# Half chunks and a split root at the head, recurrence gating on GpSimd, a last half scaled from PSUM: a two-layer hybrid diffusion backbone on one core

## The chip, the cores and the metric

The kernel runs on one core of a Trainium2 chip. The metric is device microseconds of one execution on that core, the median of several runs. The program's core has TensorE (PE) for matrix products, VectorE (DVE), ScalarE (ACT), GpSimd (POOL) and SyncE (SP); here SP only issues the transfers. Everything is fp32 in and out.

## The reference, cut to what matters

512 latent tokens and 256 context tokens of width 1024 pass through two layers, and the latent tokens are normalised at the end:

```python
for layer in range(2):
    shift, scale, gate = split(silu(c) @ ada_w[layer] + ada_b[layer])        # and the same for c_ctx
    h_l = rmsnorm(x, norm_g[layer]) * (1 + scale) + shift                    # h_c likewise
    if layer == 0: y_c, y_l = even_mixer(h_c, h_l)   # latent attention | bidirectional RG-LRU
    else:          _,   y_l = odd_mixer(h_c, h_l)    # neighbourhood attention
    x = x + gate * y_l                                                       # cx likewise in layer 0
return rmsnorm(x, final_norm_g)

# even_mixer: z = h @ w_in -> cq, ckv, k_rope, gate_mla, x_lru, gate_lru
q, k, v = heads(rmsnorm(cq) @ w_uq), heads(rmsnorm(ckv) @ w_ukv), ...        # rope on a part of q and k
u = short_conv(x_lru); a, w = coeffs(u); r = scan_forward(a, w) + scan_backward(a, w)
y = concat(attend(q, k, v) * silu(gate_mla), r * silu(gate_lru)) @ w_out
# odd_mixer: q, k, v, g = split(h @ w_in); 8x16 window + context, then (o * silu(g)) @ w_out
```

## The kernel before, in words

Activations stand transposed: a tile holds 128 of the 1024 channels for 768 tokens, the 512 latent ones first (`LAT`), the 256 of the context behind them (`CTX`). Every fp32 product is made of three products of rounded parts: a value is split into a high part (an ACT copy, `h`) and the rest (a DVE subtraction, `l`), and `h·h`, `h·l`, `l·h` are summed in PSUM. `split_w` loads a weight (`r`) and makes `h` and `l`. A recording layer and a scheduler set the order of instructions on each engine; the text of the program gives priorities, and `behind()` makes an instruction stand after the last one recorded for TensorE.

Five places of the program are touched.

The head. `x_load` brings in eight tiles of x (384 KB each). `norm0` squares them on ACT, sums the squares on DVE in `acc`, multiplies by ones on TensorE (`pssum`), takes the root on ACT (`r0t`) and a Newton step on DVE (`r0r`, L302 to L306), spreads the result over partitions by six transposes (`r0b`) and copies it to SBUF (`rsb`). Meanwhile `ada_go(ch)` computes shift and scale of two channel tiles at a time from four loads of 512 KB (`ada_0r`, `ada_4r`; TensorE `psada`, ACT `rows`, TensorE `psc`, DVE `av`, `as`, `am`). `hb(j, c)` then makes the normalised `hh`, `hl` of tile j: x·am·rsb on DVE (L330), the high part on ACT (L332), the rest on DVE (L333). The first products with the layer's weights (`psx`, `w0t0`) use them.

Layer 0's middle. `lru_x`, `lru_conv`, `lru_gates` and `lru_scan` are the recurrence for four blocks `ft`, `natural` makes cq, ckv and k_rope (`psn`, weights `w0n0` to `w0n3`), and `ada_gate(0, 0)`, called as `g00`, makes half of the layer's output gate (`psada` again). `lru_out(ft)` multiplies the gate `mix` by the recurrence: the context part contiguous (L584), the latent part in two strided views (L586). `gate_t` makes such a gate (L445 and L446).

Keys and values of layer 0. `prep_q` and `prep_kv` load and split `wq0`, `wq1` and `wkv`, `rope_q` turns q (`rb` by a shuffle, `ra`, a product on GpSimd at L712, a sum at L713, the parts `qrh` and `qrl`), `k_rope` makes the rotated key `kh`, `kl` (L670 to L673), `v_t` the values (`psv`, L689), `proj_k` the keys (`psk`).

The start of layer 1. `v_t1`, `q1` and `g1` make values, queries and gates; `prep1("w1g", 0)` loads and splits the gate's first weight. `pskl` are the keys.

The tail. The last output product (`w1oy`, L1144) is added to x (`out_add`, L1150), squared (L1697) and summed, for two halves of 256 tokens. `norm2(half)` makes the root `r2` and its spread copy `rsb2`, `finish(half)` multiplies and issues the output's transfers on SP (L1671 to L1674). Half 0's tiles have been multiplied by the final weight before (L1699); of half 1, those in `GF`.

## Time and profile before

| what | value |
|---|---|
| runs | 790.94 us median of 3 (790.9 to 793.72) |
| the profiled execution | 792.74 us, of which the span is 790.9 us |
| PE busy | 742.5 us, 94% of the span |
| DVE, ACT, POOL busy | 511.1, 415.4, 151.7 us |
| chain that ended last | PE 78%, DVE 11%, ACT 5%, issue 2%, DMA 2% |
| granted TensorE clock, mean | 0.991 |

The span is the time from the first to the last instruction; the execution's own time has 1.84 us more. An engine's busy time is summed over its instructions; the chain is followed back from the last instruction to what released each. Of TensorE's clock the profile gives the granted share, 1.00 for 2.4 GHz and 0.50 for 1.2 GHz.

### The profile page before, as it was taken

The numbers are of one execution on the slowest core, as the hardware profiler recorded it, in microseconds if no ns is written. First come the engines' busy times: TensorE is split into PE (matmuls) and PEld (weight loads), VectorE is DVE, ScalarE is ACT, GpSimd is POOL, SyncE is SP. The second block draws the span as 40 slices with busy tenths as digits, with TensorE's granted clock in tenths as the row PEclk, the third lists the DMA queues.
The fourth block names the chain that finished last, engine by engine and source line by source line (L and its number), as shares of the span: only waits on it lengthen the run. The fifth ranks groups of instructions, "written<-read, shape, count | busy, mean of one in ns | idle before, by whom it ended". The sixth has DMA issues, their size and how long they took to land.

```text
span 790.9 us, 13125 instructions
## 1 busy us (share of the span) xinstructions
PE 742.5 (94%) x4934; PEld 651.9 (82%) x4934; DVE 511.1 (65%) x1055; ACT 415.4 (53%) x806; POOL 151.7 (19%) x177
## 2 busy tenths in 40 slices
...
GB/s 326 407 43 107 63 116 102 159 42 0 110 144 148 179 166 143 96 158 273 28 80 107 80 160 15 89 112 187 56 79 156 165 107 54 124 89 164 78 1 107
DMA packets 33599, 95.29 MB, mean 120 GB/s; under 512 B 4608, under 2 KB 6784, under 8 KB 33536
## 3 DMA queue, kind: packets, MB, share of 16 engines
...
q14 instruction: 24, 0.20, 0.1%
...
## 4 chain that ended last, share of the span: by engine, by line
PE 78%; DVE 11%; ACT 5%; issue 2%; DMA 2%; SPq 1%; DVEq 0%; ACTq 0%
PE psg L140 11%; PE psv L1239 8%; PE w0oy L1144 7%; PE psq L140 6%; PE w1oy L1144 6%; PE pskl L140 6%; PE psx L140 4%; PE pt L1356 4%; PE pskc L140 3%; PE psn L611 3%; PE psada L210 2%; PE s L1315 2%; PE s L777 2%; PE s L1316 2%; PE po L1339 2%
## 5 line engine op out<-in xcount | busy, mean ns | idle before, releaser
L733 POOL TENSOR_SCALAR p<-p,rc 128x512 f32<-128x512 f32 (+1 forms) x96 | 77.7, 812 | 335.1 <-DVE rc L732 319.1
L1323 ACT ACTIVATE p<-s,nm 128x512 f32<-128x512 f32 x64 | 43.8, 686 | 36.4 <-DVE nm L1321 20.2
L1359 DVE TENSOR_TENSOR ptl<-pt,pth 128x512 fp32r<-128x512 f32 x64 | 43.7, 687 | 26.8 <-ACT pth L1358 26.8
L1358 ACT ACTIVATE pth<-pt 128x512 fp32r<-128x512 f32 x64 | 37.3, 595 | 34.8 <-PE pt L1356 25.6
L1321 DVE CUSTOM_DVE_ANT_1 s<-s,bias 128x512 f32<-128x512 f32 x48 | 33.2, 696 | 16.3 <-PE s L1316 16.1
L1356 PE MATMUL pt<-ident,p 128*128 128x128 f32 x256 | 40.0, 272 | 0.0
L813 DVE TENSOR_TENSOR pt<-pt,pt 128x512 fp32r<-128x512 f32 x48 | 31.8, 680 | 11.5 <-ACT pt L812 11.2
L712 POOL TENSOR_TENSOR rb<-rb,ropet 128x512 f32<-128x512 f32 x2 | 2.6, 1287 | 186.9 <-DVE rb L710 186.9
L812 ACT ACTIVATE pt<-pt 128x512 fp32r<-128x512 f32 x48 | 27.4, 595 | 16.1 <-PE pt L850 15.9
L732 DVE RECIPROCAL rc<-rs 128x1 f32<-128x1 f32 x96 | 15.2, 158 | 31.4 <-ACT p L1323 22.0
L1315 PE MATMUL s<-k,q 128*128 128x256 f32 x128 | 34.2, 292 | 0.6 <-ACT mix L1298 0.5
L210 PE MATMUL psada<-ada_0r,c 128*32 128x256 f32 x192 | 19.9, 407 | 15.7 <-DMA ada_0r<-ada 15.7
L781 ACT ACTIVATE p<-s,nm 128x768 f32<-128x768 f32 x32 | 28.8, 901 | 10.6 <-DVE nm L779 10.4
L1356 PEld LDWEIGHTS pt<-ident,p 128*128 128x128 f32 x256 | 31.1, 140 | 4.0 <-issue 0.4
L779 DVE TENSOR_REDUCE nm<-s 128x1 f32<-128x768 f32 x32 | 30.4, 951 | 4.7 <-PE s L777 4.3
L1316 PE MATMUL s<-k,q 128*128 128x256 f32 x128 | 33.3, 284 | 0.0
L1339 PE MATMUL po<-pth,v 128*128 128x256 f32 (+1 forms) x96 | 31.6, 336 | 0.0
L1340 PE MATMUL po<-ptl,v 128*128 128x256 f32 (+1 forms) x96 | 29.5, 324 | 0.0
L850 PE MATMUL pt<-ident,p 128*128 128x128 f32 x192 | 28.7, 274 | 0.0
L831 PE MATMUL po<-pt,v 128*128 128x256 f32 x96 | 26.1, 296 | 1.8 <-DVE pt L813 1.6
L830 PE MATMUL po<-pt,v 128*128 128x256 f32 x96 | 26.6, 294 | 0.4 <-DVE rcc L732 0.4
L1315 PEld LDWEIGHTS s<-k,q 128*128 128x128 f32 x128 | 24.3, 190 | 3.1 <-issue 1.0
...
## 6 DMA issues: line engine op xcount, KB each, us to landing
...
```

Of the source, the lines that this page charges most:

```text
L140: P.matmul(ps, a(k), b[k][:, c], start=(k == 0 and i == 0), stop=(k == nk - 1 and i == 2),)
L210: P.matmul(ps[32 * j : 32 * j + 32, :256], c34[:, k, 2 - 2 * m : 34 - 2 * m], raw[k // step][:, k % step], start=(m == 0 and k < 4), stop= ...
L733: G.tensor_scalar(p, p, rc, 0.5, ALU.mult, ALU.mult)
L1144: P.matmul(ps, a, b[k][:, c], start=(n == m == 0 and ps is dst[0][0]), stop=(n == 7 and m == 2), skip_group_check=True,)
L1239: P.matmul(ps, tok(a[k], t), b[:, k % 4], start=(k == 0 and i == 0), stop=(k == 7 and i == 2))
L1315: P.matmul(s[:, :256], lhs, kap, start=(i == 0), stop=False, skip_group_check=True)
L1316: P.matmul(s[:, 256:], lhs, k2[:, CTX], start=False, stop=(i == 1), skip_group_check=True)
L1323: S.activation(p, s, AF.Exp, bias=nm, scale=-1.0, accum_out=rsum)
L1339: P.matmul(dst, vv, h, start=first, stop=False, skip_group_check=True)
L1356: P.transpose(ps[:, 128 * j : 128 * j + 128], p1[hd, b][:, 128 * c : 128 * c + 128], ident)
L1358: S.activation(h, ps, AF.Copy)
L1359: V.tensor_tensor(l, ps, f(h), ALU.subtract)
```

## The change

At the head the first two channel tiles get their shift and scale each by itself, from a new input array `ada0` that holds the same weights in halves of 128 columns; the sum of squares and the root are made for the latent and the context tokens apart, the latent ones first (`r00`, `r01`); and a root of one column that nothing uses stands among the squares. The gate chunk `g00` is called earlier, around `lru_gates(0)`. The multiplications of `lru_out`, the sum in `rope_q` and a copy in `k_rope` go from DVE to GpSimd, and `prep_kv` stands ahead of `prep_q(0)`. In layer 1, `prep1("w1g", 0)` stands ahead of one `v_t1` and of the query weight. In the tail half 0 is finished on GpSimd alone and its eight products with the final weight are made on ACT behind its root; half 1 reads its spread root from PSUM on DVE; a root that nothing uses stands ahead of the tail; `finish` follows each `norm2`, and the odd tiles' transfers of half 1 are issued by ACT.

```diff
...
     V.tensor_scalar(badd, col(V_ADAB, 48), 1.0, None, ALU.add)
-    def behind():
-        e = next(i for i in reversed(nc.cur_bb.bb.instructions) if i.engine == mybir.EngineType.PE)
-        return tc.issue_after(e)
-    def ada_mm(raws, pp, name):
+    def behind(*engines):
+        stack = ExitStack()
+        for e in engines:
+            stack.enter_context(tc.issue_after(next(i for i in reversed(nc.cur_bb.bb.instructions) if i.engine == e)))
+        return stack
+    def ada_mm(raws, pp, name, wd=256):
...
-                    ps[32 * j : 32 * j + 32, :256], c34[:, k, 2 - 2 * m : 34 - 2 * m], raw[k // step][:, k % step],
+                    ps[32 * j : 32 * j + 32, :wd], c34[:, k, 2 - 2 * m : 34 - 2 * m], raw[k // step][:, k % step],
...
-    def ada_rows(l, ch, raws, pp, pin):
-        with behind() if pin else nullcontext():
+    def ada_rows(l, j, raws, pp, pin, na=2):
+        wd = 128 * na
+        with behind(PE) if pin else ExitStack():
...
-        with behind() if pin else nullcontext():
-            for i in range(2):
+        with behind(PE) if pin else ExitStack():
+            for i in range(na):
...
-    def ada_cols(l, ch, raws, pp, pin=False):
+    def ada_cols(l, j, raws, pp, pin=False, n=2):
...
         V.scalar_tensor_tensor(y, t, 1.5, y, ALU.add, ALU.mult)
-    def rs_bc(name, ps, n, dst, pp, root=True):
+    def rs(name, ps, n, root=True):
         nt = n // 128
         s, r = ps[:, 0 : 2 * nt : 2], small("st", f"{name}r", nt)
-        if root:
-            rsqrt1(r, s, 1.0 / D, nt, name)
-        else:
-            rsqrt(r, s, 1.0 / D, nt, "st", name)
+        (rsqrt1 if root else lambda *a: rsqrt(*a[:4], "st", a[4]))(r, s, 1.0 / D, nt, name)
+        return r
+    def bc(name, r, n, dst, pp):
         b = pp(f"{name}b")
-        for i in range(nt):
+        for i in range(n // 128):
             P.transpose(b[:, 128 * i : 128 * i + 128], r[:, i : i + 1].to_broadcast([128, 128]), ident)
         S.activation(dst[:, :n], b[:, :n], AF.Copy)
+        return b[:, :n]
+    def rs_bc(name, ps, n, dst, pp, root=True):
+        return bc(name, rs(name, ps, n, root), n, dst, pp)
     def halves(ap):
...
     rsb0 = px.tile([128, NT], F32, name="rsb0")
+    acc0 = px.tile([128, NT], F32, name="acc0")
+    root = cst.tile([128, 1], F32, name="root")
     def norm0():
-        acc = th("acc0")
-        ps = zz3("pssum")
+        sq = {}
         for j in range(8):
-            sq = th(f"sq{j}")
-            S.activation(sq, x_tiles[j], AF.Square)
-            if j == 0:
-                prev = sq
-            else:
-                V.tensor_tensor(acc, prev if j == 1 else acc, sq, ALU.add)
-        sq_sum(ps, acc, NT, True, True)
-        rs_bc("r0", ps, NT, rsb0, zz3)
+            sq[j] = th(f"sq{j}")
+            S.activation(sq[j], x_tiles[j], AF.Square)
+            if j == 4:
+                S.activation(root, sq[0][:, 0:1], AF.Sqrt)
+            for w in (LAT, CTX) if j == 7 else (slice(0, NT),):
+                if j:
+                    V.tensor_tensor(acc0[:, w], (acc0 if j > 1 else sq[0])[:, w], sq[j][:, w], ALU.add)
+                if j == 7:
+                    c = w is CTX
+                    n, pp = (NL, NC)[c], (zz, zz3)[c]
+                    ps = pp(f"pssum{c}")
+                    sq_sum(ps, acc0[:, w], n, True, True)
+                    if c == 0:
+                        rs_bc("r00", ps, n, rsb0[:, w], pp)
+                    else:
+                        norm0c = lambda: rs_bc("r01", ps, n, rsb0[:, CTX], pp)
+        return norm0c
     wt = {}
...
     def ada_go(ch):
-        for _ in ada_cols(0, ch, [ada_w.pop(ch), ada_w.pop(ch + 4)], paa):
+        for _ in ada_cols(0, 2 * ch, [ada_w.pop(ch), ada_w.pop(ch + 4)], paa):
+            pass
+    def ada_prep1(j):
+        ada_w["half", j] = [[load_w(f"ada0{j}{m}", A["ada0"][j, m], (8, 128), t4a)] for m in range(2)]
+    def ada_go1(j):
+        for _ in ada_cols(0, j, ada_w.pop(("half", j)), paa, n=1):
             pass
...
         x_load(j)
-    ada_prep(0)
-    ada_prep(4)
-    norm0()
+    ada_prep1(0)
+    norm0c = norm0()
     hh = [th(f"hh{j}", F32R) for j in range(8)]
     hl = [th(f"hl{j}", F32R) for j in range(8)]
-    ada_prep(1)
-    ada_go(0)
+    raw0 = load_w("w0t0", A["w0t"][0], (8, 128))
+    ada_prep1(1)
+    ada_go1(0)
     hb(0, 0)
-    prep_t(0)
-    hb(0, 1)
+    norm0c()
+    with behind(PE, ACT):
+        wt[0] = kfun(split_raw("w0t0", raw0, (8, 128)))
+        hb(0, 1)
+        ada_prep(1)
+        ada_go1(1)
+    hb(1, 0)
+    hb(1, 1)
     ada_prep(5)
-    hb(1, 0)
     ada_prep(2)
     ada_go(1)
-    hb(1, 1)
     ada_prep(6)
...
         g, r = mix[4 + ft], lru_s.pop(ft)["r"]
-        V.tensor_tensor(g[:, CTX], g[:, CTX], r[:, :NC], ALU.mult)
+        G.tensor_tensor(g[:, CTX], g[:, CTX], r[:, :NC], ALU.mult)
         for a, b in zip(in_cols(g), in_rows(r[:, NC:])):
-            V.tensor_tensor(a, a, b, ALU.mult)
+            G.tensor_tensor(a, a, b, ALU.mult)
     def lru_sqrt(i):
...
         S.activation(KH[1][64:96], f(KH[0][64:96]), AF.Copy)
-        V.tensor_copy(KL[1][64:96], f(KL[0][64:96]))
+        G.tensor_copy(KL[1][64:96], f(KL[0][64:96]))
     def prep_kv():
...
         G.tensor_tensor(rb[:, :NL], rb[:, :NL], ropet[0][:, 1], ALU.mult)
-        V.tensor_tensor(ra[:, :NL], ra[:, :NL], rb[:, :NL], ALU.add)
+        G.tensor_tensor(ra[:, :NL], ra[:, :NL], rb[:, :NL], ALU.add)
         S.activation(ra[:, NL:], psa[:, NL:NT], AF.Copy)
...
     lru_conv(1)
+    go("g00", ada_gate(0, 0, tt))
     lru_gates(0)
+    go("g00")
     lru_x(2, x_t(2))
     lru_gates(1)
-    go("g00", ada_gate(0, 0, tt))
-    go("g00")
     lru_conv(2)
...
     lru_scan(2)
+    prep_kv()
     prep_q(0)
...
     rope_q(0)
-    prep_kv()
     k_rope()
...
     v_t1(0, 1)
+    prep1("w1g", 0)
     v_t1(0, 2, st)
...
     q1(0, st)
-    prep1("w1g", 0)
     g1(0)
...
         return pe.tile([128, 256], F32, tag=tag, name=name, bufs=bufs)
-    GF = (1, 4, 6)
+    GF = (2, 6)
     steps = ((0, 0), (0, 2), (0, 4), (0, 6), (1, 0), (1, 2), (1, 4), (1, 6))
+    S.activation(root, p1[15, 3][:, 0:1], AF.Sqrt)
     acc2 = [etmp(f"acc2{half}", "acc", 2) for half in range(2)]
...
             if half == 0 or j in GF:
-                (V if half == 0 and j % 2 else G).tensor_tensor(x, x, rsb2[half], ALU.mult)
+                G.tensor_tensor(x, x, rsb2[half], ALU.mult)
             else:
-                V.scalar_tensor_tensor(x, x, col(V_FG + j), rsb2[half], ALU.mult, ALU.mult)
-            SY.dma_start(out[128 * j : 128 * j + 128, c], x)
+                V.scalar_tensor_tensor(x, x, col(V_FG + j), rb2[half], ALU.mult, ALU.mult)
+            (S if half and j % 2 else SY).dma_start(out[128 * j : 128 * j + 128, c], x)
+    rb2 = {}
     def norm2(half):
...
         sq_sum(pss[half], sq2[half], 256, False, True)
+        yield
+        r = rs(f"r2{half}", pss[half], 256)
+        if half == 0:
+            with behind(ACT):
+                for j in range(8):
+                    S.activation(x2[j][:, :256], x2[j][:, :256], AF.Copy, scale=col(V_FG + j))
         rsb2[half] = etmp(f"rsb2{half}", "rsb", 2)
-        rs_bc(f"r2{half}", pss[half], 256, rsb2[half], tt)
+        rb2[half] = bc(f"r2{half}", r, 256, rsb2[half], oo)
+        finish(half)
     sq2 = {}
...
             dst[1] = (st("w1oy71")[:, :256], 1)
-        for d in [[d] for d in dst] if (half, j0) == (1, 6) else [dst]:
-            out_mm(d, w1o[j0 // 2], mh, ml, [0, 3, 5, 2, 4, 1, 6, 7], c)
+        ks = [0, 3, 5, 2, 4, 1, 6, 7]
+        if (half, j0) == (1, 6):
+            for d in dst:
+                with behind(PE):
+                    out_mm([d], w1o[3], mh, ml, ks, c)
+                next(n2, None)
+        else:
+            out_mm(dst, w1o[j0 // 2], mh, ml, ks, c)
         for ps, i in dst:
...
             S.activation(sq, x2[j][:, c], AF.Square)
-            if half == 0 or j in GF:
+            if half and j in GF:
                 S.activation(x2[j][:, c], x2[j][:, c], AF.Copy, scale=col(V_FG + j))
             if 0 < j < 7:
-                (V if half else G).tensor_tensor(acc, acc, sq, ALU.add)
+                (V if half or j > 3 else G).tensor_tensor(acc, acc, sq, ALU.add)
         sq2[half] = sq
-        if (half, j0) == (1, 2):
-            norm2(0)
-    finish(0)
-    norm2(1)
-    finish(1)
+        if (half, j0) == (1, 4):
+            n2 = norm2(0)
+            next(n2)
+    for _ in norm2(1):
+        pass
     while pools:
...
     A["ada"] = ada_w.reshape(2, 8, 128, 12, 256).transpose(0, 3, 2, 1, 4)
+    A["ada0"] = ada_w[0].reshape(8, 128, 3, 8, 128)[:, :, :2, :2].transpose(3, 2, 1, 0, 4)
     def cols(a):
...
```

Three places of the resulting order. The first is TensorE's, in the products of `lru_gates` (`pg`, weights `lgh` and `lgl`) and of `natural` (`psn`). Before:

```order
L140 MATMUL pg_708<-ul_625,lgh_658 128x256
L140 MATMUL pg_708<-uh_624,lgl_660 128x256
L611 MATMUL psn_946<-w0n0l,hh_188 128x416
L611 MATMUL psn_946<-w0n0h,hl_196 128x416
L140 MATMUL pg_779<-uh_652,lgh_774 128x512
L140 MATMUL pg_779<-ul_653,lgh_774 128x512
```

and of the change:

```order
L141 MATMUL pg_756<-uh_664,lgl_708 128x256
L215 MATMUL psada_16_767<-ada_8_0r,c_109 32x256 x4
L215 MATMUL psada_16_767<-ada_8_4r,c_109 32x256 x4
L215 MATMUL psada_16_767<-ada_9_0r,c_109 32x256 x4
L215 MATMUL psada_16_767<-ada_9_4r,c_109 32x256 x4
L141 MATMUL pg_846<-uh_692,lgh_841 128x512
L141 MATMUL pg_846<-ul_693,lgh_841 128x512
```

The gate chunk's products (`psada_16`) now stand right ahead of the first product with the second block's `lgh`; before they stood some 60 rows further on. The second place is DVE's, from the gate of block 2 to the values; here `mix_1773` before and `mix_1813` in the change are the gate of block 3 (`gate_t(11, 7)`), `mix_1695` and `mix_1735` that of block 2. Before:

```order
L584 TENSOR_TENSOR mix_1695<-mix_1695,la_1229 128x256
L586 TENSOR_TENSOR mix_1695<-mix_1695,la_1229 128x8x48
L586 TENSOR_TENSOR mix_1695<-mix_1695,la_1229 128x8x16
L124 TENSOR_TENSOR wkvl<-wkvr,wkvh 128x1024
L446 SCALAR_TENSOR_TENSOR mix_1773<-mix_1773,psg_1724 128x768
L658 SCALAR_TENSOR_TENSOR cql_1806<-pscq_1814,vec,cqh_1805 128x256
L710 STREAM_SHUFFLE rb_1833<-psqr_1819 128x512
L711 TENSOR_TENSOR ra_1832<-psqr_1819,ropet 128x512
L584 TENSOR_TENSOR mix_1773<-mix_1773,la_1325 128x256
L586 TENSOR_TENSOR mix_1773<-mix_1773,la_1325 128x8x48
L586 TENSOR_TENSOR mix_1773<-mix_1773,la_1325 128x8x16
```

and of the change, on DVE:

```order
L477 SCALAR_TENSOR_TENSOR mix_1735<-mix_1735,psg_1686 128x768
L689 SCALAR_TENSOR_TENSOR cql_1751<-pscq_1752,vec,cqh_1750 128x512
L689 SCALAR_TENSOR_TENSOR cql_1751<-pscq_1759,vec,cqh_1750 128x256
L125 TENSOR_TENSOR wq1l<-wq1r,wq1h 128x512
L477 SCALAR_TENSOR_TENSOR mix_1813<-mix_1813,psg_1764 128x768
L689 SCALAR_TENSOR_TENSOR cql_1852<-pscq_1853,vec,cqh_1851 128x512
L689 SCALAR_TENSOR_TENSOR cql_1852<-pscq_1860,vec,cqh_1851 128x256
L741 STREAM_SHUFFLE rb_1879<-psqr_1865 128x512
L742 TENSOR_TENSOR ra_1878<-psqr_1865,ropet 128x512
```

and on GpSimd, where before only the product of `rb` stood at this place:

```order
L615 TENSOR_TENSOR mix_1735<-mix_1735,la_1269 128x256
L617 TENSOR_TENSOR mix_1735<-mix_1735,la_1269 128x8x48
L617 TENSOR_TENSOR mix_1735<-mix_1735,la_1269 128x8x16
L615 TENSOR_TENSOR mix_1813<-mix_1813,la_1365 128x256
L617 TENSOR_TENSOR mix_1813<-mix_1813,la_1365 128x8x48
L617 TENSOR_TENSOR mix_1813<-mix_1813,la_1365 128x8x16
L743 TENSOR_TENSOR rb_1879<-rb_1879,ropet 128x512
L744 TENSOR_TENSOR ra_1878<-ra_1878,rb_1879 128x512
L704 CAST kl_1892<-kl_1891 32x768
```

The six products of the two blocks left DVE, and on GpSimd they stand ahead of the two operations of the rope. The third place is DVE's in the tail, where `x_8058` before and `x_8098` in the change hold the last two tiles. Before:

```order
L1150 SCALAR_TENSOR_TENSOR x_8058<-w1oy_8635,ag_117,x_8058 128x256
L1701 TENSOR_TENSOR acc_8211<-acc_8211,sq_8686 128x256
L1671 TENSOR_TENSOR x_8049<-x_8049,rsb_8563 128x256
L1671 TENSOR_TENSOR x_8052<-x_8052,rsb_8563 128x256
L1671 TENSOR_TENSOR x_8055<-x_8055,rsb_8563 128x256
L1671 TENSOR_TENSOR x_8058<-x_8058,rsb_8563 128x256
L1150 SCALAR_TENSOR_TENSOR x_8058<-w1oy_8636,ag_117,x_8058 128x256
```

and of the change:

```order
L1181 SCALAR_TENSOR_TENSOR x_8098<-w1oy_8653,ag_119,x_8098 128x256
L1748 TENSOR_TENSOR acc_8252<-acc_8252,sq_8742 128x256
L1181 SCALAR_TENSOR_TENSOR x_8098<-w1oy_8654,ag_119,x_8098 128x256
L305 TENSOR_SCALAR r21m<-pss_8749 128x2
L306 RECIPROCAL r21r<-r21t 128x2
```

Half 0's four products no longer stand between the last sum of squares and the last tile's addition.

## Rows read from the trace of the kernel before

**Rows 1.** Windows by stage: length, busy us (instructions) of each engine, PEclk, DMA share, GB/s.

```profile
80.00:100.00 20.00, 17.18 (x113) 13.86 (x112) 11.96 (x17) 16.24 (x26) 0.00 (x0) 1.00 0.26 85
...
180.00:200.00 20.00, 15.40 (x75) 12.31 (x74) 18.87 (x30) 9.22 (x15) 1.28 (x1) 0.91 0.11 28
...
440.00:748.00 308.00, 307.05 (x2058) 275.45 (x2057) 187.45 (x406) 155.62 (x327) 53.35 (x68) 1.00 0.35 107
...
770.00:791.00 21.00, 8.91 (x69) 8.33 (x67) 11.35 (x29) 5.61 (x13) 6.00 (x7) 0.74 0.29 101
```

**Rows 2.** Timeline of PE at the head: start, length, instruction, idle before and releaser.

```profile
25.61 0.79 PE L140 MATMUL psx<-hh,w0t0h 128*128 128x512 f32 x2 [0.56 <-ACT hh L332]
...
35.78 0.50 PE L140 MATMUL psx<-hh,w0t0h 128*128 128x512 f32 x1
```

**Rows 3.** Timeline of ACT at the head.

```profile
19.36 1.28 ACT L301 ACT_TABLE_LOAD   x1 [4.37 <-PE pssum L290]
```

**Rows 4.** Timeline of DVE at the head.

```profile
24.05 2.20 DVE L330 SCALAR_TENSOR_TENSOR x<-x,am,rsb 128x512 f32<-128x512 f32 x4
...
32.13 2.20 DVE L330 SCALAR_TENSOR_TENSOR x<-x,am,rsb 128x512 f32<-128x512 f32 x4
```

**Rows 5.** Timeline of PE from 80 to 100 us.

```profile
86.03 0.50 PE L140 MATMUL pg<-uh,lgh 128*128 128x512 f32 x1 [0.92 <-ACT lgh L532]
...
91.26 0.65 PE L611 MATMUL psn<-w0n1h,hh 128*128 128x416 f32 x2 [0.96 <-ACT w0n1h L120]
```

**Rows 6.** Timeline of SP: the transfer of the second of `natural`'s weights.

```profile
86.73 0.33 SPq L114 DMA_DIRECT2D w0n1r<-w0n  x1
```

**Rows 7.** Timeline of PE from 182 to 200 us.

```profile
187.47 0.58 PE L140 MATMUL psk<-cqh,wkvh 128*128 128x512 f32 x2 [1.97 <-DVE mix L446]
...
195.14 0.50 PE L689 MATMUL psv<-wkvh,cqh 128*128 128x512 f32 x1 [2.13 <-DVE kl L671]
```

**Rows 8.** Timeline of DVE from 183 to 193 us.

```profile
183.77 0.42 DVE L584 TENSOR_TENSOR mix<-mix,la 128x256 f32<-128x256 f32 x1
184.11 1.22 DVE L586 TENSOR_TENSOR mix<-mix,la 128x384 f32<-128x384 f32 x2
185.24 1.22 DVE L124 TENSOR_TENSOR wkvl<-wkvr,wkvh 128x1024 fp32r<-128x1024 f32 x1
186.37 0.95 DVE L446 SCALAR_TENSOR_TENSOR mix<-mix,psg 128x768 f32<-128x768 f32 x1
...
191.75 0.68 DVE L713 TENSOR_TENSOR ra<-ra,rb 128x512 f32<-128x512 f32 x1
```

**Rows 9.** GpSimd's groups by line and shape: busy us, mean ns, idle before.

```profile
L1671 POOL TENSOR_TENSOR x<-x,rsb 128x256 f32<-128x256 f32 x7 | 6.0, 885 | 12.8 <-ACT rsb L319 12.8
...
L1701 POOL TENSOR_TENSOR acc<-acc,sq 128x256 f32<-128x256 f32 x6 | 4.4, 740 | 21.2 <-ACT sq L1697 20.8
L712 POOL TENSOR_TENSOR rb<-rb,ropet 128x512 f32<-128x512 f32 x2 | 2.6, 1287 | 186.9 <-DVE rb L710 186.9
```

**Rows 10.** Window from 196 to 200 us, columns as in rows 1.

```profile
196.00:200.00 4.00, 4.00 (x14) 3.15 (x13) 3.94 (x7) 2.84 (x5) 0.00 (x0) 0.57 0.55 137
```

**Rows 11.** Waits of PE from 400 to 440 us: total us, times, longest.

```profile
PE pskl L140 <- DVE v L1243: 1.4, 1, 1.4
PE psg L140 <- ACT w1g0h L120: 1.0, 1, 1.0
```

**Rows 12.** Timeline of DVE in the tail.

```profile
776.25 3.02 DVE L1671 TENSOR_TENSOR x<-x,rsb 128x256 f32<-128x256 f32 x4 [0.74 <-ACT rsb L319]
779.19 0.47 DVE L1150 SCALAR_TENSOR_TENSOR x<-w1oy,ag,x 128x256 f32<-128x256 f32 x1
...
783.53 3.56 DVE L1673 SCALAR_TENSOR_TENSOR x<-x,vec,rsb 128x256 f32<-128x256 f32 x5 [1.20 <-ACT rsb L319]
```

**Rows 13.** Timeline of ACT in the tail.

```profile
775.83 0.39 ACT L319 ACTIVATE rsb<-r20b 128x256 f32<-128x256 f32 x1 [0.24 <-PE r20b L318]
779.70 0.42 ACT L1697 ACTIVATE sq<-x 128x256 f32<-128x256 f32 x1 [3.48 <-DVE x L1150]
```

More of the change, by code (lines that the diff above doesn't have):

```diff
@@ L1 @@
-from contextlib import nullcontext
+from contextlib import ExitStack
 import numpy as np
@@ L52, in build @@
     V, S, P, G, SY = nc.vector, nc.scalar, nc.tensor, nc.gpsimd, nc.sync
+    PE, ACT, DVE = mybir.EngineType.PE, mybir.EngineType.Activation, mybir.EngineType.DVE
     def f(ap):
@@ L177, in build @@
     ctt = cst.tile([128, 8, 2], F32, name="ctt")
+    eps = cst.tile([128, 1], F32, name="eps")
+    G.memset(eps, EPS)
     S.activation(ctt, ct, AF.Tanh, scale=0.5)
```

32 lines of the change are left out of this document (15 added, 17 removed).

## The prediction

> **What bounds the kernel now.** I read the windows by stage first, to see where TensorE is not full, since the change takes nothing from its products. From 440 to 748 us it is busy 307.05 of 308 us, but it idles 2.82 of 20 us from 80 to 100, 4.60 from 180 to 200, and 12.09 of the last 21 [rows 1]. Time can only come from such gaps and from the head. So I then read, stretch by stretch, the timeline of PE with the releaser of each wait. At the head the first product with a weight starts at 25.61, and tile 2's at 35.78, after which no wait stands out [rows 2]; what goes before is the root, with a table load of 1.28 us in its chain [rows 3], and DVE, which starts on x at 24.05 [rows 4]. From 80 to 100 PE waits 0.92 us for a gate weight and 0.96 for `w0n1h` [rows 5], whose load is issued only at 86.73 [rows 6]. From 180 to 200 it waits 1.97 us for the gate of block 3 and 2.13 for `kl` [rows 7], and there DVE is busy 18.87 of 20 us [rows 1]: each is late because DVE works off a queue. At layer 1's start there are two waits, of 1.4 and 1.0 us [rows 11]. In the tail the last tile's addition runs at 779.19, behind four products of half 0 that take 3.02 us beside GpSimd [rows 12].
>
> **The sum is made against the profiled execution**, 792.74 us, which is 790.9 us of span and 1.84 around it. The median of the runs shown is 1.80 us below it, and I subtract the same gains from the median.
>
> **The head.** Until the first product two loads of 512 KB are wanted instead of four, and two small chains `av`, `as`, `am` replace one. The table load, 1.28 us [rows 3], goes ahead of the squares, where ACT waits for x. The latent sum needs eight of twelve products, and its copy has 512 columns instead of 768. If all of it reached the path, PE would start 2.5 us earlier. But DVE starts on x at 24.05 and is full until it starts on tile 2 at 32.13, 8.1 us later [rows 4]; the second small chain puts about 1 us more into that queue. With the new order and the old durations I get the first product at 24.0 instead of 25.61, tile 2's at 34.8 instead of 35.78, and some 0.2 us given back at the next shift and scale, which has less work ahead of it. Gain **0.8**, between 0.2 and 2.5.
>
> **The gate chunk.** 32 products of `psada`, 1.9 us by my count of its rows' starts, now stand ahead of the products with the second `lgh`, so they cover the 0.92; the load of `w0n1` no longer waits for the chunk's place in memory, which covers the 0.96 [rows 5, 6]. Of the stage's 2.82 us the rest is two waits for ACT of about 0.5 each. The chunk's sum holds one of three PSUM places of `pg` until ACT has copied it, which I put at 0.9 given back, and the stage's small waits go as well. On SP its four loads stand ahead of the next `lgr` loads, which wait for their places anyhow. Gain **1.7**, between 0 (the PSUM place costs as much as is saved) and 2.8 (all the idle time).
>
> **The gating on GpSimd.** Ahead of the gate of block 3 DVE no longer does block 2's three products, 183.77 to 185.24, and one `cql` of about 0.65 moves behind it; `wkvl` stays ahead, only earlier. The multiplication moves from 186.37 to about 184.2 and ends at 185.1 [rows 8], before PE is at `psk`, so that the wait of 1.97 goes. The second wait decides, because everything behind it moves with `kl`. GpSimd can start on block 2 when DVE ends that block's gate. Between that and block 3's stand two `cql` and `wq1l` (about 1.7), so at about 182.5. Then stand six products, the product of `rb` and the sum of `ra`. GpSimd takes 0.74 us for 256 columns and 1.29 for 512 [rows 9], which makes a contiguous block 0.74 + 1.0 + 0.46 = 2.2. No row shows it on strided views. DVE takes 0.42 for the contiguous 256, and 1.22 for the 512 strided, where it takes 0.68 contiguous [rows 8], partly from the GpSimd beside it; with 1.5 for the strided part the block is 2.9, and 3.5 when 0.74 grows to 0.885 as in the tail [rows 9]. I take 2.9, between the ends. The sum of `ra` is then at 182.5 + 2 × 2.9 + 2 × 1.29 = 190.9, where DVE's now ends at 192.43 [rows 8]. From there to `psv` at 195.14 are 2.71 us of `qrh`, `qrl` and `kl`, which stay, so `psv` starts at 193.6. Gain **1.5**; 2.5 with 2.2 us for a block (the shuffle then decides), 0.3 with 3.5. The copy of `kl` on GpSimd has nobody waiting soon; with that cover gone it costs under 1 us.
>
> The Trainium skill (GPSIMD Engine Reference, section 4.1, Engine selection) speaks against this part: two-input elementwise work is about 2 times slower on GpSimd than on VectorE. The rows agree, 1.29 against 0.68 for 512 columns [rows 8, 9]. By twice DVE's 0.42 + 1.22 a block would be 3.3 us, the gain 0.7 instead of 1.5 and the whole 784.
>
> **Layer 1.** Splitting the gate's weight earlier meets the wait of 1.0; the wait of 1.4 for a split on DVE keeps its values' products right ahead of it [rows 11]. Work moved ahead of the query weight can be late in its place. Gain **0.6**, between -0.5 and 1.5.
>
> **The tail.** ACT's root has its table loaded in an idle stretch of ACT. Eight products with the final weight, about 0.45 each, go behind half 0's root; they and the missing table load leave the copy of `rsb` about where it is, 775.83 [rows 13], so GpSimd starts its eight products at about 775.6 and ends at 781.5 with 0.74 each, at 782.7 with 0.885 [rows 9]. DVE has lost the four products (3.02), so the last addition follows TensorE's last product at about 777, with one sum of squares that may run beside GpSimd: the square starts at 777.4 instead of 779.70 [rows 13], 2.3 earlier. From that square to DVE's first product are 3.83 us now, 779.70 to 783.53 [rows 12, 13], of which 0.4 is the copy that DVE no longer waits for: DVE starts at 780.8. Six products of about 0.45, the length of the addition that reads PSUM now [rows 12], end at 783.4. GpSimd does its two of half 1 behind the eight and ends between 783.0 and 784.4. Now DVE ends at 787.09, 3.56 after 783.53 [rows 12]. What follows, transfer and end, stays at 3.8. The gain is 2.7 to 4.1; I take **3.3**.
>
> The Trainium skill (SBUF — State Buffer, section SBUF: two separate sides) says that a VectorE operation with two SBUF inputs and a GpSimd operation that reads SBUF exclude each other for a whole instruction. The trace agrees where half 0's four products take 0.76 each beside GpSimd, and 0.42 alone [rows 8, 12]. By it `wq1l` could wait one GpSimd product, 0.74, and the sum would be about 0.3 less.
>
> **The sum.** 0.8 + 1.7 + 1.5 + 0.6 + 3.3 = 7.9. The profiled execution would go from 792.74 to 784.8, the median from 790.94 to 783.0. A measurement of this kernel tells about 0.5%, 3.95 us, from no change, so faster begins at 787.0.
>
> **The rivals.**
> *Only the tail.* The waits in the middle come back one step later: `pg` for its PSUM place, `psv` for GpSimd, the head for DVE. For it: in all three DVE or ACT stay busy. Against: in two of the three the late weight and the late gate get earlier by more than the wait. Tail 3.3 and 0.4 of the rest: 787.2. Chance 0.20.
> *The clock comes back.* From 196 to 200 us the granted clock is 0.57, for the most part at its lower level, 1.2 GHz, after PE was idle for 4.6 us of the stretch [rows 1, 10]; what it does in these 4 us takes about 1.7 us more than at 2.4 GHz (0.43 of 4). If PE's shorter waits keep it at 2.4 GHz, that is gained too, and with the head and the layer start near their upper ends, 779.5. For it: the other gaps leave the clock at 1.00 [rows 1]. Against: a wait of 1.5 to 2.5 us for `kl` remains. Chance 0.14.
> *GpSimd's strided products make it slower.* If a view of eight short rows costs GpSimd as eight operations would, a block takes far more than 2.9. `psv` starts at 187.8 + 2b: at b = 3.7 the middle gains nothing, at 6.9 all other gains (6.4) are eaten, at 8.9 it is 4 us slower, 795; with eight times the 0.74 for each view, b = 12.6 and 802. For it: DVE too is slower on these views [rows 8]. Against: that is 1.5 times and not eight. Chance 0.06.
> *It does nothing.* The tail is still bounded by GpSimd and the loads at the head take the time the root has left: 789 to 790. Against: the tail's chain is short and each piece has a row. Chance 0.04.
>
> **How the numbers follow.** My forecast, 783.0, has 0.56; its own range is 780.5 to 785.5, from the bounds of its terms. Faster is that, the clock's case and 8 of the 20 hundredths of the tail's case: 0.78. Same is the other 12 and the case of nothing: 0.16. Slower is 0.06. The range, 778.5 to 788.5, holds the first three.
>
> **What would show it.** Right: `psx` first near 24.0, tile 2's near 34.8; no wait for `lgh` and `w0n1h`; `psk` with no wait; `psv` near 193.6 less what the stages ahead gained (2.5), GpSimd's blocks at 2.9; the last square 2.3 earlier against TensorE's end, the last products on DVE near 0.45. Wrong: strided products on GpSimd above 1.5 us, a new wait of `pg` over 1 us, DVE's queue at the head longer than 8.1 + 1 us, or GpSimd ending half 0 after 783.

## The result, and the profile after

The changed kernel takes 781.91 us (median of 4 runs, 781.59 to 784.38), the kernel before 791.99 in the same measurement (4 runs, 790.9 to 793.72). The ratio is 0.9878, 95% interval 0.9848 to 0.9907: 1.2% faster, 1.1 us below the forecast of 783.0 and inside the likeliest case's own range. The profiled execution took 781.84 us with a span of 780.0, which is 10.9 less than the span of 790.9 before; the sum of the prediction was 7.9. The total is near, but several of its terms are not, in both directions.

The windows by stage, which answer to [rows 1] and [rows 10] (length, busy time and instructions of PE, PEld, DVE, ACT and POOL, granted clock, DMA share, GB/s):

```profile
80.00:100.00 20.00, 19.35 (x126) 16.59 (x124) 11.56 (x17) 15.24 (x25) 0.00 (x0) 1.00 0.40 130
...
180.00:200.00 20.00, 17.95 (x97) 14.62 (x95) 10.79 (x17) 8.47 (x15) 5.86 (x6) 1.00 0.38 90
...
440.00:748.00 308.00, 307.17 (x2079) 276.36 (x2078) 186.29 (x405) 156.25 (x328) 53.45 (x68) 1.00 0.35 105
...
196.00:200.00 4.00, 4.00 (x24) 3.44 (x24) 0.00 (x0) 0.00 (x0) 0.00 (x0) 1.00 0.91 214
```

TensorE's idle time falls from 2.82 to 0.65 us in the first stretch and from 4.60 to 2.05 in the second. DVE, which was busy for 18.87 of the 20 us from 180 to 200, is busy for 10.79. Of these 8.1 us the six products moved to GpSimd explain 4.1, and the sum and the copy 1.2; for the rest DVE's queue starts earlier, and it is empty from 194.44 on. And from 196 to 200 the granted clock is 1.00, where it was 0.57.

The timeline of PE, answering to [rows 2, 5, 7] (start, us, engine, line, operation, and in brackets the idle time before it with its releaser):

```profile
23.29 0.79 PE L141 MATMUL psx<-hh,w0t0h 128*128 128x512 f32 x2 [1.08 <-ACT hh L340]
...
34.81 0.50 PE L141 MATMUL psx<-hh,w0t0h 128*128 128x512 f32 x1
...
87.61 0.50 PE L141 MATMUL pg<-uh,lgh 128*128 128x512 f32 x1 [0.65 <-ACT rows L227]
88.51 0.65 PE L642 MATMUL psn<-w0n1h,hh 128*128 128x416 f32 x2
...
137.04 0.50 PE L141 MATMUL pg<-uh,lgh 128*128 128x512 f32 x1 [0.24 <-ACT lgh L563]
...
139.07 0.62 PE L141 MATMUL pg<-uh,lgl 128*128 128x512 f32 x2 [0.83 <-DVE lgl L565]
...
182.26 0.51 PE L141 MATMUL psk<-cqh,wkvh 128*128 128x512 f32 x2
...
189.36 0.50 PE L720 MATMUL psv<-wkvh,cqh 128*128 128x512 f32 x1 [1.42 <-DVE kl L702]
```

`psx` and tile 2 start where they were forecast, the waits for `w0n1h` and for block 3's gate are gone, and `psv` starts at 189.36 where 191.1 was foreseen. Of the gate chunk a wait of 0.65 for ACT's copy `rows` is left at 87.61, where 0.9 had been put down. New are the waits of 0.24 for `lgh` at 137 and of 0.83 for `lgl` at 139.

The tail, on GpSimd, ACT and DVE, answering to [rows 12, 13]; TensorE's last output product ends at 768.33 (776.86 before):

```profile
766.78 5.70 POOL L1703 TENSOR_TENSOR x<-x,rsb 128x256 f32<-128x256 f32 x8 [10.59 <-ACT rsb L323]
768.89 0.42 ACT L1744 ACTIVATE sq<-x 128x256 f32<-128x256 f32 x1 [1.34 <-DVE x L1181]
770.30 0.16 DVE L305 TENSOR_SCALAR r21m<-pss 128x2 f32<-128x2 f32 x1 [1.44 <-ACT r21t L304]
...
770.57 0.57 DVE L307 TENSOR_TENSOR r21t<-r21r 128x2 f32<-128x2 f32 x1
771.17 0.65 DVE L308 SCALAR_TENSOR_TENSOR r21t<-r21t,r21m 128x2 f32<-128x2 f32 x1
771.85 0.65 DVE L309 SCALAR_TENSOR_TENSOR r21r<-r21t,r21r 128x2 f32<-128x2 f32 x1
773.34 0.38 ACT L323 ACTIVATE rsb<-r21b 128x256 f32<-128x256 f32 x1 [3.07 <-PE r21b L322]
773.75 2.44 DVE L1705 SCALAR_TENSOR_TENSOR x<-x,vec,r21b 128x256 f32<-128x256 f32 x6 [1.26 <-ACT rsb L323]
```

The square follows TensorE by 0.56 us (2.84 before), so it is 2.3 earlier, as forecast. The DVE products are 0.41 apart, and GpSimd is done with half 0 at 772.5. But from the square to the first product are 4.86 us, and 3.4 were foreseen.

**Where the time came from, product by product.** The same TensorE products are found in both traces. The lead of a kernel at a product is its start in the profile of before less its start in that kernel, so each column to the next says what a stage gave. Each lead is from one profiled execution:

| kernel | 80 | 127 | 141 | 182 | 207 | 374 | 443 | 776 | span's end |
|---|---|---|---|---|---|---|---|---|---|
| after | 1.3 | 3.0 | 1.3 | 3.0 | 6.8 | 7.0 | 8.6 | 8.5 | 10.9 |
| `lruV` | 1.3 | 3.1 | 2.9 | 4.6 | 7.6 | 7.9 | 9.5 | 10.1 | 12.8 |
| `lru01V` | 1.4 | 3.2 | 3.0 | 4.6 | 8.5 | 8.2 | 9.8 | 9.8 | 12.1 |
| `g00old` | 0.9 | 0.9 | -3.3 | -2.6 | -0.7 | -1.7 | -0.1 | 0.2 | 2.9 |
| `g00lruV` | 0.3 | 0.3 | 0.3 | 0.3 | 0.8 | 0.5 | 2.1 | 2.4 | 4.7 |
| `kvold` | 1.0 | 2.8 | 1.1 | 2.7 | 5.0 | 4.4 | 6.1 | 6.0 | 8.6 |
| `l1old` | 1.4 | 3.2 | 1.7 | 3.5 | 7.3 | 7.0 | 7.0 | 7.6 | 10.2 |
| `headold` | 1.5 | 2.5 | 0.7 | 2.4 | 6.2 | 5.7 | 7.3 | 7.5 | 10.2 |
| `tailold` | 1.5 | 3.2 | 1.6 | 3.3 | 7.1 | 6.9 | 8.5 | 8.7 | 9.2 |
| `gatonly` | 0.3 | -0.6 | -2.4 | -2.1 | 0.5 | -0.4 | -0.4 | 0.0 | 0.5 |

The columns are the times in the trace of before, in us. Column by column of after: the gate chunk's stage gives 1.7 (80 to 127), something takes 1.6 back (127 to 141), 1.7 come from 141 to 182, the stage of q, k and v gives 3.8 (182 to 207), layer 1's start 1.6, the tail 2.4. A lead also changes when other products pass from one side of the product looked at to the other. That is so at 141: up to 182 TensorE waits 0.15 us in before and not at all in after, and the 1.7 are work that after has done earlier. Of the 1.6 that after loses before it, the two new waits are 1.07.

### The profile page after: what moved, and what is told of

It reads as the page before. It is cut to its first block, busy times and chain, and to the rows that moved or that the text cites. A ratio compares the mean times of both kernels' runs of the same rounds, so it can differ in the third digit from the quotient of the medians.

```text
span 780.0 us, 13217 instructions
## 1 busy us (share of the span) xinstructions
PE 740.8 (95%) x4966; PEld 652.3 (84%) x4966; DVE 507.5 (65%) x1050; ACT 415.1 (53%) x810; POOL 164.8 (21%) x192
## 4 chain that ended last, share of the span: by engine, by line
PE 75%; DVE 11%; ACT 5%; issue 3%; DMA 3%; SPq 1%; POOL 0%; DVEq 0%; ACTq 0%; POOLq 0%
PE psg L141 10%; PE psv L1270 8%; PE w0oy L1175 7%; PE psq L141 6%; PE w1oy L1175 6%; PE pskl L141 6%; PE psx L141 4%; PE pt L1387 3%; PE pskc L141 3%; PE s L808 3%; PE s L1346 2%; PE psada L215 2%; PE s L1347 2%; PE po L1370 2%; PE po L1371 2%
## 5 line engine op out<-in xcount | busy, mean ns | idle before, releaser
L615 POOL TENSOR_TENSOR mix<-mix,la 128x256 f32<-128x256 f32 x4 | 3.6, 888 | 171.8 <-DVE la L609 123.6
L763 DVE RECIPROCAL rc<-rs 128x1 f32<-128x1 f32 x96 | 15.2, 158 | 32.7 <-ACT p L1354 23.6
L1200 ACT ACTIVATE sq<-xr 128x512 f32<-128x512 f32 (+1 forms) x16 | 8.2, 522 | 33.1 <-DVE xr L1181 27.1
```

## The experiments

Unless said otherwise each kernel is the changed one with one edit, and the times are medians.

**One: the tail, and the gating in half and whole.** `tail3` gives three of half 0's tiles to DVE, and half 0's spread root takes its place in PSUM from another pool:

```diff
+    D0 = (1, 3, 5)
+    GFS = (tuple(j for j in range(8) if j not in D0), GF)
...
-            if half == 0 or j in GF:
+            if j in GFS[half]:
                 G.tensor_tensor(x, x, rsb2[half], ALU.mult)
...
-                for j in range(8):
+                for j in GFS[0]:
                     S.activation(x2[j][:, :256], x2[j][:, :256], AF.Copy, scale=col(V_FG + j))
...
-        rb2[half] = bc(f"r2{half}", r, 256, rsb2[half], oo)
+        rb2[half] = bc(f"r2{half}", r, 256, rsb2[half], oo if half else tt)
```

> The changed kernel, but of half 0's eight closing products DVE makes three (tiles 1, 3, 5) from the spread root in PSUM, GpSimd five. Theory (a GpSimd instruction holds up DVE's two-column operations that touch SBUF alone, so that the last root's five steps took 2.2 us instead of 0.86): GpSimd is done about 3 products, 2.1 us, earlier, near the time at which the last root begins, the five steps return to about 0.9 us, and the end comes 1.0 to 1.4 us earlier than in the changed kernel, near 780.7. Rival (the steps are slow for another reason, or GpSimd's two products of half 1 set the end anyway): the steps stay above 1.8 us or the end moves by less than 0.4 us.

Measured 779.78 us (778.89 to 781.25), ratio 0.9851 (0.9833 to 0.9868), 2.1 below after; the slowest of its four runs, 781.25, is under the fastest of after, 781.59. DVE's timeline of `tail3`:

```profile
772.07 0.16 DVE L307 TENSOR_TENSOR r21t<-r21r 128x2 f32<-128x2 f32 x1
772.27 0.16 DVE L308 SCALAR_TENSOR_TENSOR r21t<-r21t,r21m 128x2 f32<-128x2 f32 x1
772.46 0.16 DVE L309 SCALAR_TENSOR_TENSOR r21r<-r21t,r21r 128x2 f32<-128x2 f32 x1
773.63 2.44 DVE L1707 SCALAR_TENSOR_TENSOR x<-x,vec,r21b 128x256 f32<-128x256 f32 x6 [1.00 <-ACT rsb L323]
```

The root's five small steps take 0.82 us here, 2.20 in after. In `tail3` GpSimd was done with its five products at 771.16, ahead of the chain; in after it ran until 772.5, and steps beside it take 0.57 to 0.65, near the 0.71 of one of its products (5.70 for 8). So GpSimd's products, though nobody waits for them, stretched the chain that ends the program. Of the 2.1 us these steps are 1.4; the transposes behind them take 0.40 for 0.66, and from DVE's last product to the end are 3.39 us for 3.85.

`tailold` has the whole tail of before:

> The changed kernel with the tail of the kernel before (from the last output products on). Theory (the tail is worth 2.4 us by the ledger of leads, not the 3.3 predicted): the end comes 2.2 to 2.6 us later than in the changed kernel, near 784.3, and the lead over the kernel before at the last output product stays 8.5. Rival (the tail is worth the 3.3 that was predicted, and one undisturbed pair of profiles misjudged it by chance): 3.0 to 3.6 us later, near 785.2.

Measured 784.02 us (783.31 to 784.53), ratio 0.9902 (0.9887 to 0.9917). The new tail is worth 2.1 us in medians and 2.4 by the leads of after.

`lru01V` and `lruV` put `lru_out` back on DVE, for blocks 0 and 1 or for all:

```diff
+        E = V if ft < 2 else G
-        G.tensor_tensor(g[:, CTX], g[:, CTX], r[:, :NC], ALU.mult)
+        E.tensor_tensor(g[:, CTX], g[:, CTX], r[:, :NC], ALU.mult)
...
-            G.tensor_tensor(a, a, b, ALU.mult)
+            E.tensor_tensor(a, a, b, ALU.mult)
```

> The changed kernel, with the gating of blocks 0 and 1 back on DVE and that of blocks 2 and 3 on GpSimd. Theory (the lead of 1.7 us that the gate chunk wins by 127 us is lost again by 140 us because GpSimd's products of blocks 0 and 1 stretch DVE's small operations beside them from 0.16 to as much as 1.3 us, which makes the last low part of a gate weight late): TensorE's wait of 0.8 us for that low part near 139 us is gone, the lead at 140 us is 2.2 to 3.0 us instead of 1.3, and the end is up to 1 us earlier, 781 to 782. Rival (the lead is lost to the order of TensorE's work or to ACT's table loads in that stretch, and is made up by 164 us in either kernel): the lead at 164 us stays at 2.4 to 2.5 and the end stays within 0.4 us of the changed kernel.

> The changed kernel with all four blocks' gating back on DVE (the sum of the rope and the copy of the keys stay on GpSimd). Theory (moving the gating off DVE is what removed TensorE's wait for block 3's gate and shortened the one for the low keys, and by that let the clock stay up): a wait of 1 to 2 us for that gate comes back near 183 us, the wait for the low keys grows past 1.4 us, the clock falls again after it, and the end is 2 to 4 us later, 784 to 786. Rival (the earlier key and value weight and the order around it removed the waits, and the gating itself is worth nothing there): the end is within 0.7 us of the changed kernel.

`lru01V` took 780.28 us (779.49 to 780.96), ratio 0.9855 (0.9840 to 0.9870), and `lruV` 780.42 (779.91 to 780.87), ratio 0.9859 (0.9843 to 0.9875). So my theory for `lruV`, that the gating of blocks 2 and 3 on GpSimd is what carries the gain near 190 us, fell: without any gating there the kernel is not slower but 1.5 us faster than after, and all eight runs of `lru01V` and `lruV` are faster than the fastest of after. The two differ by the gating of blocks 2 and 3 alone: on GpSimd it gives 0.9 at 207 (8.4 against 7.5), and 0.1 is left of it in the medians, within their spread. What the gating cost is seen at blocks 0 and 1, between 127 and 141. GpSimd and DVE in after:

```profile
125.20 1.34 POOL L615 TENSOR_TENSOR mix<-mix,la 128x256 f32<-128x256 f32 x1 [123.61 <-DVE la L609]
126.51 1.82 POOL L617 TENSOR_TENSOR mix<-mix,la 128x384 f32<-128x384 f32 x2
...
130.52 1.88 POOL L617 TENSOR_TENSOR mix<-mix,la 128x384 f32<-128x384 f32 x2
...
125.84 0.73 DVE L283 TENSOR_SCALAR nn1t<-nn1m 128x4 int32<-128x4 int32 x1
126.60 1.23 DVE L284 TENSOR_SCALAR nr<-nn1t 128x4 int32<-128x4 int32 x1
...
130.53 1.34 DVE L288 TENSOR_TENSOR nn1t<-nr 128x4 f32<-128x4 f32 x1
131.90 0.51 DVE L289 SCALAR_TENSOR_TENSOR nn1t<-nn1t,nn1m 128x4 f32<-128x4 f32 x1
...
138.32 0.69 DVE L565 TENSOR_TENSOR lgl<-lgr,lgh 128x512 fp32r<-128x512 f32 x1
```

And DVE in `lru01V` at the same place:

```profile
125.59 0.17 DVE L283 TENSOR_SCALAR nn1t<-nn1m 128x4 int32<-128x4 int32 x1
125.67 0.42 DVE L616 TENSOR_TENSOR mix<-mix,la 128x256 f32<-128x256 f32 x1
126.00 1.29 DVE L618 TENSOR_TENSOR mix<-mix,la 128x384 f32<-128x384 f32 x2
127.22 0.15 DVE L284 TENSOR_SCALAR nr<-nn1t 128x4 int32<-128x4 int32 x1
...
135.52 0.69 DVE L565 TENSOR_TENSOR lgl<-lgr,lgh 128x512 fp32r<-128x512 f32 x1
```

Operations on four columns take 0.51 to 1.34 us beside GpSimd and about 0.16 without it, so taking 1.7 us of products a block off DVE did not make its queue shorter, and the last `lgl` comes 2.8 us later. Its place in DVE's fixed order is part of that: in after six more steps of the roots, about 0.2 each, stand ahead of it. That `lgl` is the 0.83 that TensorE waits at 139; in `lru01V` it does not wait between 100 and 145.

**Two: each of the other moves undone.** `kvold` has `prep_kv` back behind `rope_q(0)`, `l1old` has `prep1("w1g", 0)` back behind `q1(0, st)`, `headold` the head of before, and `g00old` the chunk back:

```diff
-    go("g00", ada_gate(0, 0, tt))
     lru_gates(0)
-    go("g00")
     lru_x(2, x_t(2))
     lru_gates(1)
+    go("g00", ada_gate(0, 0, tt))
+    go("g00")
```

> The changed kernel with the split of the key and value weight back at its old place, behind the turned queries. Theory (GpSimd's gating and the earlier weight work together: the weight's low part takes 1.1 us of DVE ahead of block 3's gate and the turned queries if it stands late): a wait of about 1 us comes back between 180 and 190 us, and the end is 0.7 to 2.5 us later than in the changed kernel, 782.6 to 784.4; more if the clock falls. Rival (the gating alone freed DVE): no wait beyond those of the changed kernel, the end within 0.4 us.

> The changed kernel with the gate chunk back at its old place. Theory (the 1.7 us that the chunk wins by 127 us are lost by 140 us, because a wait further on bounds that stretch in either kernel): TensorE's waits for the gate weight and for the second weight of the natural projections, about 0.9 us each, are back between 80 and 100 us, but the lead at 140 us is within 0.4 us of the changed kernel's 1.3, and the end within 0.6 us of it. Rival (the chunk's 1.7 us reach the end, as was predicted): 1.3 to 2.1 us later, near 783.6.

> The changed kernel with the split of layer 1's first gate weight back behind the queries. Theory (the layer's start is worth the 1.6 us that the ledger of leads shows, because the wait for a value's split, 1.4 us, went as well as that for the gate weight): the end is 1.3 to 1.9 us later, near 783.5, and both waits are back. Rival (only the wait for the gate weight hangs on this, and the value's split was early for another reason): 0.5 to 1.0 us later.

> The changed kernel with the head of the kernel before (double chunks, one root over all tokens, no early table load). Theory (the head is worth the 1.2 us that stand in the ledger from 57 us on): the lead at 57 us is 0 and the end is 0.9 to 1.5 us later, near 783.1. Rival (a later stage would have taken up the lead in any case, as it does at 140 us): the end within 0.4 us of the changed kernel.

`kvold` took 785.03 us (783.37 to 786.25), ratio 0.9921 (0.9901 to 0.9941): 3.1 later than after, more than was expected with the clock up. Two of its four runs, 783.37 and 784.14, have a mean granted clock of 0.995 and 0.994, the other two, 785.92 and 786.25, 0.992; between the profiled executions it is 2.3. Its leads fall behind those of after from 182 on (5.0 against 6.8 at 207); the load of `wkv` is issued at 167.92, `psv` waits 1.66 us for `v` on DVE at 190.35 (1.42 for `kl` in after), and its clock is 1.00 from 196 to 200.

`l1old` took 782.91 (782.54 to 783.94), ratio 0.9895 (0.9880 to 0.9909). Its leads have no gain from 374 to 443, where after has 1.6, and TensorE has two waits there again, 0.97 for `w1g0h` and 1.36 for `v`, which answer to those of [rows 11]. `headold` took 782.41 (781.39 to 782.76), ratio 0.9884 (0.9869 to 0.9899), and its runs overlap with those of after. Its lead at 57 us is 1.5 with the old head. TensorE's first product, which waits for the first transfer, starts at 15.54 in the profile of before and between 13.96 and 15.2 in those of the other kernels: that spread is as large as the head's whole term, and the head's own worth, 0 to about 0.5, can't be told from it. Counted from each kernel's own first product, nothing of the head's gain is left at 57 us: after's lead there, 1.0, is its earlier first product (1.03), while in `headold` 0.3 of the 1.5 remain.

`g00old` took 789.01 (9 runs, 787.48 to 790.03), ratio 0.9969 (0.9959 to 0.9979): 7.1 us later. Both theories of its expectation fell. TensorE waits 2.45 us for `tg` in it (ACT does two squares ahead of the gate's table load and waits 3.97 us for DVE in front of them), but that is one wait; by the leads it loses 4.2 between 127 and 141 and has not got back what after gains at 207.

**Three: why the chunk is worth so much, and whether the moves do anything alone.** `g00lruV` has the chunk back and all gating on DVE, so that it differs from `lruV` by the chunk's place alone. `kvonly` and `gatonly` are the kernel before with the early `prep_kv` alone, and with the gating, the sum of `ra` and the copy of `kl` on GpSimd alone. `best` is `lru01V` and `tail3` together.

> The changed kernel with the gate chunk at its old place and all gating on DVE. Theory (the 7 us lost by the chunk's old place with gating on GpSimd came from ACT's order: two squares that wait for DVE stood ahead of block 1's gate; with gating on DVE they stand behind it): no wait of 2.5 us near 134 us, the lead at 142 us is about the head's, 0.7 to 1.5 us, and the end is 1.5 to 2.5 us later than in the kernel with the chunk early and all gating on DVE (780.4), so 782 to 783. Rival (the chunk's place itself costs the 7 us through its transfers or its PSUM place): near 787 again.

> The kernel before with one edit: the key and value weight is loaded and split ahead of the query weights. Theory (this move, not the gating on GpSimd, carries most of what the middle gained): the wait of 2.0 us for block 3's gate goes or shrinks below 0.7, the clock stays at its upper level from 196 to 200 us, and the end is 2 to 4 us earlier than in the kernel before, 787.5 to 789.5. Rival (it needs the gating to leave DVE): less than 1 us.

> The kernel before with the gating of all blocks, the rope's sum and the copy of the keys on GpSimd, and nothing else. Theory (alone, the gating costs more at blocks 0 and 1, where it stretches DVE's small operations and puts two of ACT's squares ahead of a gate, than it saves at blocks 2 and 3): the lead at 142 us is 2 to 5 us below zero, about 2 come back by 200 us, and the end lies between the kernel before and 3 us later. Rival (as predicted, GpSimd's share shortens the middle by 1.5 us): 1 to 2 us earlier.

> The changed kernel with both mends that the runs before point to: blocks 0 and 1 gated on DVE again, and three of half 0's closing products on DVE from PSUM. Theory (the two are worth 1.3 us at the last output product and 2.0 us behind it, and lie in different stages): they add up, the end is 2.8 to 3.6 us earlier than in the changed kernel, near 778.6. Rival (the tail's gain hangs on where the chain before it ends, or one of the two was the spread of the first transfers): less than 2 us together.

`g00lruV` took 787.82 (787.22 to 788.85), ratio 0.9952 (0.9937 to 0.9967), 7.4 later than `lruV`: the size comes again without GpSimd, so my theory, that most of the loss of `g00old` came from its meeting with GpSimd's gating, fell, and the rival's number came. One chain of loads, splits and products differs in the two traces. In `lruV`, on PE, SP, DVE and ACT (`psn` are `natural`'s products):

```profile
83.73 0.64 PE L215 MATMUL psada<-ada_0r,c 128*32 128x256 f32 x8
...
84.43 0.33 SPq L115 DMA_DIRECT2D w0n1r<-w0n  x1
...
85.97 0.33 SPq L115 DMA_DIRECT2D w0n3r<-w0n  x1
...
92.16 1.02 DVE L125 TENSOR_TENSOR w0n3l<-w0n3r,w0n3h 128x832 fp32r<-128x832 f32 x1 [0.34 <-ACT w0n3h L121]
...
93.22 0.33 SPq L561 DMA_DIRECT2D lgr<-lrug  x1
...
99.58 0.68 DVE L565 TENSOR_TENSOR lgl<-lgr,lgh 128x512 fp32r<-128x512 f32 x1
...
106.06 0.51 PE L141 MATMUL pg<-uh,lgh 128*128 128x512 f32 x2
106.40 0.35 PE L642 MATMUL psn<-w0n0h,hh 128*128 128x416 f32 x1
...
133.50 0.62 ACT L563 ACTIVATE lgh<-lgr 128x512 fp32r<-128x512 f32 x1
...
156.35 2.77 ACT L621 ACTIVATE lm<-lm 128x3072 f32<-128x3072 f32 x1
```

and in `g00lruV`:

```profile
95.59 0.64 PE L215 MATMUL psada<-ada_0r,c 128*32 128x256 f32 x8
...
96.29 0.33 SPq L115 DMA_DIRECT2D w0n3r<-w0n  x1
...
101.52 0.33 SPq L561 DMA_DIRECT2D lgr<-lrug  x1
...
108.77 0.69 DVE L565 TENSOR_TENSOR lgl<-lgr,lgh 128x512 fp32r<-128x512 f32 x1
...
118.55 0.35 PE L642 MATMUL psn<-w0n3h,hl 128*128 128x416 f32 x1
118.74 0.39 PE L141 MATMUL pg<-uh,lgh 128*128 128x512 f32 x1
...
140.41 0.62 ACT L563 ACTIVATE lgh<-lgr 128x512 fp32r<-128x512 f32 x1
...
163.33 2.77 ACT L621 ACTIVATE lm<-lm 128x3072 f32<-128x3072 f32 x1
```

The chunk's four loads go out between 59.05 and 62.76 in `g00lruV`; in `lruV` one goes out at 37.20 and three near 59. Loaded weights of several kinds share a few places in memory (`t4`). The chunk holds its places until its products `psada` are made, at 83.73 or only at 95.59. By SP's waits the load of `w0n1` waits for these products in `lruV`, and the third load of a gate weight (`lgr`, block 2's) in both kernels for `w0n3l`, which gives its place back; in `g00lruV` the load of `w0n3` waits for the chunk's products instead. With the chunk's products early, `w0n3` is loaded 10.3 us sooner, the third `lgr` 8.3, block 2's gate products begin 12.7 and block 3's split 6.9 sooner. ACT's last root of the recurrence (L621) starts at 156.35 instead of 163.33; in after it is 157.87, in before 163.63. DVE's products behind it start as much earlier (159.15 against 166.13), and DVE has room from 180 to 200 (busy 10.66 us against 16.43). In `g00lruV` TensorE waits 1.84 us for `wq1l` at 186.11 and its granted clock falls below 1.00 between 184 and 192; none of that is in `lruV`. By the leads the distance of the two grows by 1.7 us from 80 to 127, by 1.4 to 182 and by 2.5 to 207, where 1.7 is what the clock took (0.90 and 0.67 over 4 us each). The waits of SP show the links up to the third `lgr`. The next one is no wait: TensorE idles nowhere from 100 to 180 us in `lruV` and for 0.16 us in all in `g00lruV`, and there block 2's `lgl` has been ready for 9.3 us when its products begin. What differs is TensorE's fixed order: in `lruV` block 2's first products stand ahead of 48 of `natural`'s 144 (`psn`), in `g00lruV` behind all of them. The scheduler set that order beforehand; that it did so because of the places is not shown, and no kernel moved the loads of `w0n1` to `w0n3`, or that order, alone.

`kvonly` took 792.21 (10 runs, 790.14 to 793.61), ratio 1.0006 (0.9996 to 1.0016): the move that costs 3.1 us when it is undone gains nothing alone, and the number of its expectation's rival came. `wq1l` is then late at 185.33 (1.84), and the granted clock is 0.68 from 184 to 188. `gatonly` took 792.24 (10 runs, 790.82 to 797.03), ratio 1.0017 (1.0000 to 1.0033): as expected, no gain. Its leads show why in one row: it loses 2.7 us from 80 to 141 and has it back at 207.

`best` took 778.93 (777.95 to 780.74), ratio 0.9841 (0.9826 to 0.9856). Its span is 777.2; the two savings, 1.6 and 2.1, add up to within 0.8. By its median it is the fastest of these kernels, 3.0 us below after; its runs overlap with those of `tail3` and `lru01V`.

## Why the prediction was right in its total, and where its steps failed

**The head (0.8).** The step came as it was worked out, `psx` at 23.29 (24.0 foreseen) and tile 2 at 34.81 (34.8). But 1.0 of the 2.3 at `psx` is the later first transfer in the profile of before, 15.54 against 14.51, and `headold` shows no more than 0.5, within the spread of the runs. The term was too high; the range's lower end, 0.2, is nearer.

**The gate chunk (1.7).** The local sum came: the lead grows from 1.3 to 3.0 between 80 and 127, and the wait for its place in PSUM is 0.65 (0.9 foreseen). The step that failed is "On SP its four loads stand ahead of the next `lgr` loads, which wait for their places anyhow". They do wait for places, but for those that the splits of `w0n1` to `w0n3` give back, and I had let only `w0n1` come earlier and only for its own wait of 0.96. In after the third `lgr` goes out at 92.63 instead of 101.62, and block 2's products stand earlier in TensorE's order. Undone, the chunk costs 7.1 to 7.4 us and not 1.7: the largest error of the prediction.

**The gating on GpSimd (1.5).** The step that failed is the gain itself. `psk` did lose its wait and blocks 2 and 3 took 2.53 us each (2.9 foreseen), so the rival of 795 to 802 is out. The strided views did cost GpSimd something: 1.32 and 0.58 us for 384 and 128 columns, where 1.0 and 0.46 were reckoned for contiguous ones. But DVE had room at 185 through the earlier recurrence, and for blocks 2 and 3, which alone I had costed, `lru01V` against `lruV` leaves 0.1 of the 1.5. At blocks 0 and 1, which I did not cost at all, GpSimd held up DVE's small operations (1.6 us by the leads and by `lru01V`), so that taken back whole the gating gives 1.5. The sum of `ra` and the copy of `kl` stayed on GpSimd in these kernels; no run undoes them by themselves. The Trainium skill (SBUF — State Buffer, section SBUF: two separate sides) gives an exclusion of this kind; I weighed it for one subtraction only, at 0.3. By it a short operation with two SBUF inputs can cost a whole GpSimd product, and the rows agree: 0.65 in place of 0.16 in the tail beside products of 0.71. Two readings of the working were off as well: the 1.22 of DVE's strided views at 184.11 owe nothing to GpSimd, which starts only at 188.52, and against 0.68 they are 1.8 times and not 1.5. That the sum of the terms came near is luck: by the undone moves +5.4 on the chunk and -3.0 on the gating, and 3.1 for a move that had no term.

**The early `prep_kv`.** It had no term of its own ("`wkvl` stays ahead, only earlier"). Undone with the chunk early it costs 3.1 in medians (2.3 between the profiled executions), and alone it gives nothing: I take it that DVE must first have room, which `kvonly` and `kvold` fit but do not isolate.

**The rival "the clock comes back" (0.14)** did happen: 1.00 from 196 to 200, which by [rows 10] is about 1.7 us. Its total of 779.5 did not come: it wanted the head near its upper end as well. What kept the clock up is open: a wait of 1.42 for `kl` remained, and in `gatonly` the clock is 1.00 from 184 to 200 with a wait of 2.63 for `v` at 195.74.

**Layer 1 (0.6).** 1.6 by the leads, 1.0 by medians. I gave nothing for the wait of 1.4 for a split on DVE; it went too; one of 0.7 that was there before stays, and one of 0.5 for `w1q0h` is new.

**The tail (3.3).** 2.4. The square 2.3 earlier, the products at 0.41 and the 3.8 behind them came as said. Two terms were missed: the five small steps stretched from 0.82 to 2.20 beside GpSimd (1.4), and the 0.4 for the copy, which DVE still waits for: its products, which read PSUM, start 0.41 after that copy begins.

The moves are not a sum. Undone one at a time they come to 7.1 + 3.1 + 2.1 + 1.0 + 0.5 - 1.5 = 12.3 us, and the whole change gives 10.1 in medians.
